# Two-tile feed-forward boundary and transferred head parts in a two-layer fp32 kernel on one core

## The chip, the cores and the metric

The kernel is one program on one core of a Trainium2 chip. Its five instruction streams are TensorE (PE: matmuls, with weight loads shown apart as PEld), VectorE (DVE), ScalarE (ACT), GpSimd (POOL) and SyncE (SP, which here only starts transfers). Each takes its instructions in the order in which they stand in its queue. The metric is the device time of one execution in microseconds, the median of the runs.

## The reference

Two layers over 512 tokens of width 1024, batch 1, in fp32:

```
for layer in 0, 1:
    a = rmsnorm(h, g); mem_n = rmsnorm(mem, g)              # mem: 256 rows
    layer 0: main = gelu(u) * spatial(layernorm(gelu(v)))   # u, v, q_mem = a @ w_in_a; 128-token chunks, 6 groups
    layer 1: k, v, log_f = rmsnorm(h, g) @ w_shared_kv      # 12 heads of 64, causal, blocks of 128 queries
             p = softmax(q k^T / 8 + c_t - c_s), c = cumsum(log_sigmoid(log_f + b)); main = p v
    memory:  4 heads of 64 attend to the 256 rows of mem_n @ w_mem_kv
    h = h + rmsnorm(concat(main, memory) @ w_out, g)
    f = rmsnorm(h, g)
    h = h + rmsnorm((silu(f @ w_gate) * (f @ w_up)) @ w_down, g)   # hidden width 2816 = 22 tiles of 128
```

## The kernel before

Activations lie transposed: `h` is [128, 8, 512], eight tiles of 128 features by 512 tokens. A product in fp32 accuracy is made of three matmuls: each operand is split into a high and a low part (`split`: ScalarE casts the high part, VectorE subtracts it for the low part; with a fourth argument GpSimd subtracts instead), and `mm3` issues high·high, low·high and high·low, which are the profile's lines L174, L175 and L176. Weights come in pieces of 512 KB (`raw`, four buffers, started from SyncE's queue) and are split into `whi` and `wlo` (eight buffers each). PSUM accumulators have three buffers under the tag mm, three under lg, two under tr.

A scheduler orders each engine's queue by the program's text and by when buffers come free. The stages follow each other: layer A's mixing; a boundary; layer A's feed-forward part; a boundary; layer B's projections; its 4 memory heads and 12 forgetting heads (`attend`); a boundary; layer B's feed-forward part; the end.

**A boundary** (`boundary`) ends one residual step and begins the next product. For each half of the tokens (`HALVES`, 256 columns each) it transposes the result `y` (`yt`, L738), adds it to `h` (`residual`), makes the scaled high and low parts of one tile at a time (`normed_parts`: `xshi` on ScalarE, `xslo` by L228 on VectorE), and squares a pair of tiles (`PairNorm.pair`: `sq`, L292, and additions, L294). `Norm.finish` forms the mean square of each token by matmuls of a squared tile with a column `avg` (`st`, L265) and GpSimd raises it to the power -1/2 (`r`, L237). `spread` broadcasts `r` by two matmuls with the identity (`rb`, L233) and copies it to `rbc` (L280). The products of the next step (`group`, accumulators `ps`) run on the unnormalised parts meanwhile; `rbc` scales their results when they are evacuated. In a feed-forward part this is `hidden` for the first two of the 22 hidden tiles: `gr` = gate × `rbc` (L958, VectorE), SiLU (L960, ScalarE), `f` = up × SiLU (L962, VectorE), and the split into `fhi` and `flo`. `close` is spread and evacuation of the second half.

**The feed-forward part** does the other 20 hidden tiles by Strassen's scheme in Winograd's form (`Seven`: seven products of quadrants for eight). `combined` makes the sums of input quadrants that it needs (t3, d2, t4 and d1), after which the first down product `y` (L174 to L176 with a moving width of 512) uses the two plain tiles `fs` with weights from `down_weights`. Before, that part is written in this order:

```
a, close = boundary(phase, G_MIX_POST + layer, G_FFN_PRE + layer, nnorm, rb, first, evac_first)
xs, last = combined(a, G_FFN_PRE + layer, xp)
close()
last()
ys = [[plain("y") for _ in range(2)] for _ in range(TB)]
w = [down_weights(layer, 0, dh) for dh in range(2)]
```

**Layer B's heads.** `Softmax.weigh` takes a block's maximum and exponential with the sum, `norm` scales one block of 128 queries (reciprocal L418, L419: `mp` for memory heads, `p` for the others), `turn` transposes blocks and splits them (`pT`), `join` puts the two heads of a pair into one tile of features (`mixed`, split head by head, L397 and L398). A forgetting head multiplies stacked operands: `qa` and `ka` hold high and low halves above each other, `qc` and `kc` the remaining parts and two rows of the cumulative bias each. `head_parts` makes them for each head from half-height tiles of `q` and `k`, with casts on ScalarE (L1185 and others) and VectorE (`qc`, L1190), subtractions on GpSimd, and two small transfers (L1179, L1180). GpSimd also subtracts for the weights of keys and values in layer B (`prepared(..., G ...)`) and for the heads' values. The keys of the memory reach the other half of the partitions by a transfer of GpSimd's queue (`memk`).

## Time and profile before

| | us |
|---|---|
| median of 3 runs (1162.25 to 1165.3) | 1164.44 |
| profiled execution, its time | 1163.55 |
| its span in the trace | 1161.8 |
| TensorE busy | 1127.2 (97%) |
| VectorE busy | 910.3 (78%) |
| ScalarE busy | 673.4 (58%) |
| GpSimd busy | 89.8 (8%) |

Mean granted clock of TensorE: 0.992 of full speed. The stages by the time from the span's start, with TensorE's and VectorE's busy time in them: layer A's mixing 0 to 165 (156.0 and 124.7 us); boundary 165 to 225 (56.7 and 50.0); feed-forward part 225 to 535 (309.3 and 248.5); boundary 535 to 575 (39.0 and 31.7); projections of layer B 575 to 610 (35.0 and 18.6); heads 610 to 765 (144.9 and 132.3); tail of the mixing 765 to 785 (20.0 and 9.3); boundary 785 to 835 (46.7 and 41.7); feed-forward part 835 to 1140 (304.9 and 240.9); end 1140 to 1162 (14.5 and 12.4).

How the quoted rows read. A group row gives line, engine, operation, output <- inputs, partitions x elements, count (x), then busy us and mean ns of one, then idle time of the engine before it and what ended it. A window row gives start:end, its length, busy us (and count) of PE, PEld, DVE, ACT and POOL, then the granted clock, the share of the DMA engines and GB/s. A timeline row gives start and length in us, then the instructions; the bracket is the wait before them, and its releaser. In a row of transfers the last number is us from issue to landing; where it has three durations they are the issue's minimum, median and maximum in ns.

### The profile page before, as it was taken

The numbers are of one execution on the slowest core, as the hardware profiler recorded it, in microseconds if no ns is written. First come the engines' busy times: TensorE is split into PE (matmuls) and PEld (weight loads), VectorE is DVE, ScalarE is ACT, GpSimd is POOL, SyncE is SP. The second block draws the span as 40 slices with busy tenths as digits, with TensorE's granted clock in tenths as the row PEclk, the third lists the DMA queues.
The fourth block names the chain that finished last, engine by engine and source line by source line (L and its number), as shares of the span: only waits on it lengthen the run. The fifth ranks groups of instructions, "written<-read, shape, count | busy, mean of one in ns | idle before, by whom it ended". The sixth has DMA issues, their size and how long they took to land.

```text
span 1161.8 us, 19755 instructions
## 1 busy us (share of the span) xinstructions
PE 1127.2 (97%) x7485; PEld 1027.0 (88%) x7485; DVE 910.3 (78%) x1783; ACT 673.4 (58%) x1401; POOL 89.8 (8%) x96
## 2 busy tenths in 40 slices
PE   7999999999999999999998999999999999999997
PEld 6898889899899898998987887789799899899996
DVE  7989557898698587897657889857898589678775
ACT  6675466565365263567546788866666256345454
POOL 0000000000000000000024552300000000000000
PEclk9999999999999999999999999999999999999999
DMA  8313221424134223352221111121134233324222
GB/s 290 121 37 109 91 73 37 143 82 157 55 109 146 72 75 109 108 175 84 90 73 56 56 38 58 36 91 37 37 112 148 68 109 110 109 74 145 73 74 73
DMA packets 58183, 108.69 MB, mean 94 GB/s; under 512 B 4013, under 2 KB 38841, under 8 KB 58089
## 3 DMA queue, kind: packets, MB, share of 16 engines
q1 hardware_dynamic: 57624, 106.87, 28.6%
q8 instruction: 59, 0.97, 0.3%
q0 software_dynamic: 320, 0.52, 0.2%
q14 instruction: 36, 0.29, 0.1%
q10 hardware_dynamic: 144, 0.05, 0.0%
HBM read 104.71 MB, written 2.10 MB: 92 GB/s over the span
## 4 chain that ended last, share of the span: by engine, by line
PE 77%; DVE 12%; ACT 7%; issue 2%; DMA 1%; POOL 1%; POOLq 0%; DVEq 0%; ACTq 0%; SPq 0%
PE y L174 8%; PE y L176 8%; PE y L175 8%; PE a L175 4%; PE a L174 4%; PE a L176 4%; PE ps L176 3%; PE ps L175 3%; PE ps L174 3%; PE x L174 3%; PE x L175 3%; PE x L176 3%; PE e L174 3%; PE e L176 3%; PE e L175 3%
## 5 line engine op out<-in xcount | busy, mean ns | idle before, releaser
L222 ACT CAST whi<-raw 128x512 fp32r<-128x512 f32 x460 | 278.6, 620 | 278.8 <-PE y L176 110.9
L223 DVE TENSOR_TENSOR wlo<-raw,whi 128x512 fp32r<-128x512 f32 x442 | 295.3, 686 | 113.1 <-ACT whi L222 108.5
L174 PE MATMUL y<-whi,fhi 128*128 128x512 f32 x352 | 139.3, 399 | 3.8 <-DVE gr L958 2.8
L175 PE MATMUL y<-wlo,fhi 128*128 128x512 f32 x352 | 138.3, 394 | 0.5 <-DVE wlo L223 0.5
L176 PE MATMUL y<-whi,flo 128*128 128x512 f32 x352 | 138.1, 393 | 0.1
L174 PE MATMUL x<-xshi,whi 128*128 128x256 f32 x320 | 90.5, 283 | 0.0
L175 PE MATMUL x<-xslo,whi 128*128 128x256 f32 x320 | 90.5, 283 | 0.0
L175 PE MATMUL a<-xslo,whi 128*128 128x256 f32 x320 | 90.5, 283 | 0.0
L176 PE MATMUL x<-xshi,wlo 128*128 128x256 f32 x320 | 90.5, 283 | 0.0
L174 PE MATMUL a<-xshi,whi 128*128 128x256 f32 x320 | 90.5, 283 | 0.0
L176 PE MATMUL a<-xshi,wlo 128*128 128x256 f32 x320 | 90.4, 283 | 0.0
L174 PEld LDWEIGHTS y<-whi,fhi 128*128 128x128 f32 x352 | 66.8, 190 | 20.7 <-DVE gr L958 3.6
L175 PEld LDWEIGHTS y<-wlo,fhi 128*128 128x128 f32 x352 | 67.0, 190 | 14.8 <-DVE wlo L223 1.6
L176 PEld LDWEIGHTS y<-whi,flo 128*128 128x128 f32 x352 | 66.7, 190 | 15.1 <-DVE flo L223 1.1
L174 PE MATMUL ps<-xshi,whi 128*128 128x256 f32 (+1 forms) x224 | 68.5, 306 | 0.0
L176 PE MATMUL ps<-xshi,wlo 128*128 128x256 f32 (+1 forms) x224 | 67.7, 302 | 0.0
L175 PE MATMUL ps<-xslo,whi 128*128 128x256 f32 (+1 forms) x224 | 67.3, 300 | 0.0
L175 PEld LDWEIGHTS a<-xslo,whi 128*128 128x128 f32 x320 | 61.4, 192 | 0.3
L174 PEld LDWEIGHTS a<-xshi,whi 128*128 128x128 f32 x320 | 61.4, 192 | 0.3
L176 PEld LDWEIGHTS x<-xshi,wlo 128*128 128x128 f32 x320 | 61.3, 192 | 0.0
L176 PEld LDWEIGHTS a<-xshi,wlo 128*128 128x128 f32 x320 | 61.3, 192 | 0.0
L175 PEld LDWEIGHTS x<-xslo,whi 128*128 128x128 f32 x320 | 61.3, 192 | 0.0
(287 smaller groups left out, 3235.4 us busy)
## 6 DMA issues: line engine op xcount, KB each, us to landing
raw<-in_w_gate SPq DMA_DIRECT2D x44, 512.0 KB
raw<-in_w_up SPq DMA_DIRECT2D x44, 512.0 KB
raw<-in_w_down SPq DMA_DIRECT2D x44, 512.0 KB
raw<-in_w_out SPq DMA_DIRECT2D x16, 512.0 KB
raw<-in_w_b_q SPq DMA_DIRECT2D x8, 512.0 KB
raw<-in_w_a_v SPq DMA_DIRECT2D x6, 512.0 KB
raw<-in_w_a_u SPq DMA_DIRECT2D x6, 512.0 KB
raw<-in_w_v SPq DMA_DIRECT2D x6, 512.0 KB
```

Source lines behind the costliest of these rows:

```text
L174: PE.matmul(o, w[0], x[0], start=start, stop=False, skip_group_check=more)
L175: PE.matmul(o, w[0], x[1], start=False, stop=False, skip_group_check=more)
L176: PE.matmul(o, w[1], x[0], start=False, stop=stop, skip_group_check=more)
L222: A.copy(hi, src)
L223: (eng or V).tensor_sub(lo, src, hi)
```

## The change

Seven edits.

1. `PairNorm` adds all four squared pairs into one, so `finish` multiplies two squared tiles for a block of tokens instead of four.
2. The feed-forward boundaries work on two tiles at a time: ScalarE writes the scaled pair in fp32 (`hs`, two activations), then one full-width split makes its parts. Layer B's boundary keeps single tiles. In all boundaries `finish` of the second half moves between the two groups of products.
3. `down_weights` for the first down product and `close` move ahead of `combined`, and `combined` works in place on the scaled pairs, two tiles wide, with its own parts t3, d2 and t4.
4. `join` collects both heads of a pair in one fp32 tile and splits it once, full height.
5. `Softmax.norm` takes two blocks' reciprocals in one instruction and scales both then.
6. The transfer of `memk` reads and writes the same bytes as fp32.
7. In layer B the subtractions of GpSimd (weights, values, queries, keys) go to VectorE; the queries and keys of two heads are split at once (`pair_split`), and six transfers of 64x512 for each head on SyncE's queue stack the parts.

SyncE's queue goes from 234 rows to 294, GpSimd's from 89 to 35, VectorE's from 1729 to 1664, ScalarE's from 1292 to 1242, TensorE's from 7304 to 7286.

TensorE's queue in the first feed-forward boundary, where the products of the second half end (`ps`) and the first down product (`y`) begins, with the broadcast `rb` of the second half. Before:

```order
L174 MATMUL ps_2294<-xshi_1777,whi_2053 128x256
L175 MATMUL ps_2294<-xslo_1778,whi_2053 128x256
L176 MATMUL ps_2294<-xshi_1777,wlo_2054 128x256
L265 MATMUL st_2343<-avg,sq_2108 128x1 x2
L265 MATMUL st_2343<-avg,sq_2121 128x1 x2
L265 MATMUL st_2343<-avg,sq_2108 128x1 x2
L265 MATMUL st_2343<-avg,sq_2121 128x1 x2
L174 MATMUL y_2475<-whi_2457,fhi_1759 128x512
L175 MATMUL y_2475<-wlo_2458,fhi_1759 128x512
L176 MATMUL y_2475<-whi_2457,flo_1760 128x512
L233 MATMUL rb_2419<-ident,r_3_1758 128x128 x2
L174 MATMUL y_2475<-whi_2461,fhi_1761 128x512
```

After:

```order
L174 MATMUL ps_2296<-xshi_2178,whi_2038 128x256
L175 MATMUL ps_2296<-xslo_2179,whi_2038 128x256
L176 MATMUL ps_2296<-xshi_2178,wlo_2039 128x256
L233 MATMUL rb_2365<-ident,r_3_1746 128x128 x2
L174 MATMUL y_2429<-whi_2347,fhi_1747 128x512
L175 MATMUL y_2429<-wlo_2348,fhi_1747 128x512
L176 MATMUL y_2429<-whi_2347,flo_1748 128x512
```

The row sums `st` stand earlier, before the last two groups of products, and the broadcast stands ahead of the first `y` instead of behind three of its matmuls.

ScalarE's queue at the same place, around the load of the SiLU table (`whi` from `raw` are the down weights; `silu` is of the first half). Before:

```order
L292 ACTIVATE sq_2184<-h 128x512
L222 CAST whi_2457<-raw_2455 128x512
L960 ACT_TABLE_LOAD
L960 ACTIVATE silu_2229<-gr_2227 128x256
L222 CAST t_1_2362<-t_2_2364 128x256
L828 ACTIVATE b_2_2373<-h,gains 128x256
L222 CAST fhi_1759<-f_2231 128x256
L960 ACTIVATE silu_2237<-gr_2235 128x256
```

After:

```order
L292 ACTIVATE sq_2182<-h 128x512
L222 CAST xshi_2178<-hs_2175 128x512
L222 CAST whi_2347<-raw_2345 128x512
L222 CAST whi_2351<-raw_2345 128x512
L965 ACT_TABLE_LOAD
L965 ACTIVATE silu_2223<-gr_2221 128x256
L222 CAST whi_2357<-raw_2355 128x512
L222 CAST whi_2361<-raw_2355 128x512
L222 CAST fhi_1747<-f_2225 128x256
```

A second piece of the down weights stands ahead of the table load, two more right behind the first SiLU, and the casts of `combined` are gone from here.

VectorE's queue at the same place, from the copy of the second half's broadcast (`rbc`) on. Before:

```order
L280 COPY rbc<-rb_2419 128x256
L839 SCALAR_TENSOR_TENSOR td_2409<-h,minus_2355,d_2_2390 128x256
L958 TENSOR_TENSOR gr_2423<-ps_2243,rbc 128x256
L839 SCALAR_TENSOR_TENSOR t_8_2410<-h,minus_2355,td_2409 128x256
L223 TENSOR_TENSOR td_lo_2407<-td_2409,td_hi_2406 128x512
L223 TENSOR_TENSOR t_7_2408<-t_8_2410,t_7_2408 128x256
L962 TENSOR_TENSOR f_2427<-ps_2244,silu_2425 128x256
```

After:

```order
L280 COPY rbc<-rb_2365 128x256
L223 TENSOR_TENSOR t_2_2398<-hs_1955,t_1_2397 128x512
L963 TENSOR_TENSOR gr_2369<-ps_2237,rbc 128x256
L223 TENSOR_TENSOR t3lo_2404<-hs_2105,t3hi_2403 128x512
L852 SCALAR_TENSOR_TENSOR hs_1992<-hs_2175,hs_1992 128x512
L967 TENSOR_TENSOR f_2373<-ps_2238,silu_2371 128x256
```

Between `gr` and `f` stand two full-width steps of `combined` instead of one full and two half ones.

SyncE's queue in layer B, between two loads of key weights (`w_k`). Before:

```order
L135 DMA raw_8175<-in_w_k 128x1024
L135 DMA raw_8329<-in_w_k 128x1024
L1179 DMA qc_7123<-cc 2x512
L1180 DMA kc_7125<-cc 2x512
L150 DMA raw_8623<-in_w_out 128x4x256
```

After:

```order
L135 DMA raw_8121<-in_w_k 128x1024
L1194 DMA qc_7071<-whi_7642 64x512
L1194 DMA kc_7073<-wlo_7645 64x512
L1195 DMA qc_7071<-cc 2x512
L1196 DMA kc_7073<-cc 2x512
L1194 DMA qa_7666<-whi_7642 64x512
L1194 DMA qa_7666<-wlo_7643 64x512
L1194 DMA ka_7667<-whi_7644 64x512 x2
L135 DMA raw_8279<-in_w_k 128x1024
```

Each head's two bias transfers are now among eight, and the next load of key weights stands behind them.

The diff, cut to its core:

```diff
-            if j > 1:
-                V.tensor_add(self.sq[j - 2, cols], self.sq[j - 2, cols], self.sq[j, cols])
+            if j:
+                V.tensor_add(self.sq[0, cols], self.sq[0, cols], self.sq[j, cols])
...
-            return [self.sq[j, cols][:, x, c] for j in range(2) for x in range(2)]
+            return [self.sq[0, cols][:, x, c] for x in range(2)]
...
-        own, _ = rows(j)
-        f = temp("f")
+            f = joined[m] = temp("f", tag="acc", bufs=2)
+        else:
+            f = temp("f")
         A.copy(f[:64, :], o[64:, :])
-        V.tensor_add(f[own, :], o[:64, :], f[:64, :])
-        hi, lo = mixed[m]
-        def rest():
-            A.copy(hi[own, :], f[own, :])
-            V.tensor_sub(lo[own, :], f[own, :], hi[own, :])
-        return rest
+        V.tensor_add(joined[m][own, :], o[:64, :], f[:64, :])
+        if j:
+            return lambda: split(joined[m], *mixed[m])
 
...
         def norm(self, tb):
-            c, p = slice(tb, tb + 1), self.p[tb]
-            V.reciprocal(self.sm[:, c], self.sm[:, c])
-            V.tensor_scalar_mul(p, p, self.sm[:, c])
+            if tb % 2:
+                return
+            V.reciprocal(self.sm[:, tb : tb + 2], self.sm[:, tb : tb + 2])
+            for x in (tb + 1, tb):
+                V.tensor_scalar_mul(self.p[x], self.p[x], self.sm[:, x : x + 1])
 
         def turn(self, n, pieces):
...
                 for x in range(2):
-                    k = 2 * j + x
-                    residual(tr[:, 256 * x : 256 * x + 256], k, cols, post)
-                    normed_parts(pre, k, cols, *xs[k])
+                    residual(tr[:, 256 * x : 256 * x + 256], 2 * j + x, cols, post)
+                    if scaled is None:
+                        normed_parts(pre, 2 * j + x, cols, *xs[2 * j + x])
+                if scaled is not None:
+                    scaled[j, half] = plain("hs", (P, 2, 256))
+                    for x in range(2):
+                        A.activation(scaled[j, half][:, x, :], h[:, 2 * j + x, c0:c1], AF.Copy,
+                                     scale=gain(pre, 2 * j + x))
+                    xs[j, half] = pair_parts("xs", scaled[j, half])
                 nnorm.pair(j, cols)
+        def inputs(half):
+            if scaled is not None:
+                return [tuple(t[:, k % 2, :] for t in xs[k // 2, half]) for k in range(KT)]
+            c0, c1 = HALVES[half]
+            return [tuple(t[:, c0:c1] for t in xs[k]) for k in range(KT)]
...
-        outs = group(ws, xs, h0, ["mm", "lg"] * 2, lag=4,
+        outs = group(ws, inputs(0), h0, ["mm", "lg"] * 2, lag=4,
                      after={3: lambda: turn(1, range(2)), 5: lambda: turn(1, range(2, 4))})
         nnorm.finish(h0)
         nnorm.spread(h0, dst)
         evac(outs, h0)
-        outs = group(ws[:2], xs, h1, ["mm", "lg"])
-        outs += group(ws[2:], xs, h1, ["mm", "lg"])
+        outs = group(ws[:2], inputs(1), h0, ["mm", "lg"])
         nnorm.finish(h1)
+        outs += group(ws[2:], inputs(1), h0, ["mm", "lg"])
...
-    def combined(a, pre, xp):
...
-            def from_h(o, x, g, y):
-                V.scalar_tensor_tensor(out=o, in0=x, scalar=g, in1=y, op0=ALU.mult, op1=ALU.subtract)
-            from_h(f[:, 0, :], h[:, n + k, c1], gain(pre, n + k), b12)
-            from_h(d, h[:, k, c0], gain(pre, k), b12)
-            from_h(f[:, 1, :], h[:, n + k, c1], less, d)
-            from_h(f4, h[:, n + k, c0], less, f[:, 1, :])
-            split(f, hi, lo)
...
+    def pair_parts(s, src, room=None):
+        hi, lo = room or [act(f"{s}{n}", shape=(P, 2, 256)) for n in ("hi", "lo")]
+        split(src, hi, lo)
+        return hi, lo
...
+    def combined(xs, scaled, xp):
+        t3, d2, t4 = [], [], []
+        for j in range(2):
+            b11, b12, b21, b22 = (scaled[x] for x in ((j, 0), (j, 1), (j + 2, 0), (j + 2, 1)))
+            V.tensor_sub(b11, b11, b12)
+            V.tensor_sub(b12, b22, b12)
+            t3.append(pair_parts("t3", b12))
+            V.scalar_tensor_tensor(out=b22, in0=b11, scalar=-1.0, in1=b22, op0=ALU.mult, op1=ALU.subtract)
+            d2.append(pair_parts("d2", b22))
+            V.scalar_tensor_tensor(out=b21, in0=b22, scalar=-1.0, in1=b21, op0=ALU.mult, op1=ALU.subtract)
+            t4.append(pair_parts("t4", b21, [xp.tile([P, 2, 256], F32R, tag="t4", name=name("t4")) for _ in range(2)]))
 
         def end():
-            for k, d in enumerate(ones):
-                split(d, *(x[:, c1] for x in a[k]))
-        quadrant = lambda k0, c: [(x[0][:, c], x[1][:, c]) for x in a[k0 : k0 + n]]
-        return (quadrant(0, c0), t3, quadrant(n, c0), d2, t4, quadrant(n, c1), quadrant(0, c1)), end
+            for j in range(2):
+                split(scaled[j, 0], *xs[j, 1])
...
+        halves = lambda pairs: [tuple(t[:, x, :] for t in p) for p in pairs for x in range(2)]
+        quadrant = lambda j, half: halves([xs[j, half], xs[j + 1, half]])
+        return (quadrant(0, 0), halves(t3), quadrant(2, 0), halves(d2), halves(t4), quadrant(2, 1), quadrant(0, 1)), end
...
-        a, close = boundary(phase, G_MIX_POST + layer, G_FFN_PRE + layer, nnorm, rb, first, evac_first)
-        xs, last = combined(a, G_FFN_PRE + layer, xp)
+        scaled = {}
+        a, close = boundary(phase, G_MIX_POST + layer, G_FFN_PRE + layer, nnorm, rb, first, evac_first, scaled)
+        w = [down_weights(layer, 0, dh) for dh in range(2)]
         close()
+        xs, last = combined(a, scaled, xp)
         last()
...
-        w = [down_weights(layer, 0, dh) for dh in range(2)]
...
-                w.extend(prepared(i["w_k"][m], (KT, P), G if m else None))
+                w.extend(prepared(i["w_k"][m], (KT, P)))
...
-                    w.extend(prepared(i["w_v"][j, kh], (4, 256), G if j else None))
+                    w.extend(prepared(i["w_v"][j, kh], (4, 256)))
...
+        def pair_split(pr):
+            pair["q"], pair["k"] = pair_of_parts(), pair_of_parts()
+            split(qs[pr], *pair["q"])
+            split(keys[pr], *pair["k"])
...
             own, other = rows(u.j)
-            q, k = qs[u.pr], keys[u.pr]
...
             u.parts = qa, qc, ka, kc = act("qa"), qc, act("ka"), kc
...
-                A.copy(qa[own, :], q[own, :])
-                G.tensor_sub(qa[other, :], q[own, :], qa[own, :])
...
-                G.tensor_sub(kc[:64, :], k[own, :], ka[own, :])
...
-                V.tensor_copy(qc[:64, :], q[own, :])
...
+            (qh, ql), (kh, kl) = pair["q"], pair["k"]
+            for dst, src in ((qa[own, :], qh), (qa[other, :], ql), (ka[own, :], kh), (ka[other, :], kh),
+                             (qc[:64, :], qh), (kc[:64, :], kl)):
+                nc.sync.dma_start(dst.bitcast(F32), src[own, :].bitcast(F32))
+            nc.sync.dma_start(qc[66:68, :].bitcast(F32), cc[n : n + 33 : 32, :].bitcast(F32))
+            nc.sync.dma_start(kc[64:66, :].bitcast(F32), cc[64 + n : 64 + n + 33 : 32, :].bitcast(F32))
...
-                    split(src.rearrange("p a (b c) -> p a b c", b=2), dst[:, :, :, 0, :], dst[:, :, :, 1, :], G)
...
-            before[len(heads) - 1] = [ready, lambda chunks=chunks: chunks[1](), lambda chunks=chunks: chunks[2]()]
-            if j == 0:
-                before[len(heads) - 1].append(values)
...
+                    split(src.rearrange("p a (b c) -> p a b c", b=2), dst[:, :, :, 0, :], dst[:, :, :, 1, :])
+            make = lambda u=u, n=n: head_parts(u, n)
+            before[len(heads) - 1] = [make] if j else [lambda pr=pr: pair_split(pr), make, values]
```

More of the change, by code (lines that the diff above doesn't have):

```diff
@@ L363, in mem_project @@
                 if layer:
-                    G.dma_start(both[other, :, :], both[own, :, :])
+                    G.dma_start(both[other, :, :].bitcast(F32), both[own, :, :].bitcast(F32))
                 else:
@@ L772, in mix_tail, with boundary @@
         return tail_of([mixed[k] for k in ORDER[4:]], lambda kp, dh, aside: out_weights(layer, 2 + kp, dh, aside), ys)
-    def boundary(phase, post, pre, nnorm, dst, block, evac):
+    def boundary(phase, post, pre, nnorm, dst, block, evac, scaled=None):
         tail, ys = phase
-        xs = parts("xs")
         h0, h1 = HALVES
+        xs = {} if scaled is not None else parts("xs")
         def turn(half, pairs):
@@ L814, in boundary @@
         return xs, close
-    def combined(a, pre, xp):
-        n = KT // 2
-        c0, c1 = (slice(*c) for c in HALVES)
-        minus = xp.tile([P, KT], F32, tag="minus", name=name("minus"), bufs=1)
-        V.tensor_scalar_mul(minus, gains[:, pre * KT : (pre + 1) * KT], -1.0)
-        t3, d2, t4, ones = [], [], [], []
-        for k in range(n):
-            b12 = temp("b12", (P, 256), "sq", 3)
-            A.activation(b12, h[:, k, c1], AF.Copy, scale=gain(pre, k))
-            if k % 2 == 0:
-                d1 = plain("d1", (P, 2, 256))
-            d = d1[:, k % 2, :]
-            ones.append(d)
-            hi, lo = act("td_hi", shape=(P, 2, 256)), act("td_lo", shape=(P, 2, 256))
-            last = xp.tile([P, 2, 256], F32R, tag="t4", name=name("t4"))
-            f, f4 = prob("td", (P, 2, 256)), temp("t4", (P, 256), "sq", 3)
-            less = minus[:, n + k : n + k + 1]
-            def from_h(o, x, g, y):
-                V.scalar_tensor_tensor(out=o, in0=x, scalar=g, in1=y, op0=ALU.mult, op1=ALU.subtract)
-            from_h(f[:, 0, :], h[:, n + k, c1], gain(pre, n + k), b12)
-            from_h(d, h[:, k, c0], gain(pre, k), b12)
-            from_h(f[:, 1, :], h[:, n + k, c1], less, d)
-            from_h(f4, h[:, n + k, c0], less, f[:, 1, :])
-            split(f, hi, lo)
-            split(f4, last[:, 0, :], last[:, 1, :])
-            t3.append((hi[:, 0, :], lo[:, 0, :]))
-            d2.append((hi[:, 1, :], lo[:, 1, :]))
-            t4.append((last[:, 0, :], last[:, 1, :]))
-        def end():
-            for k, d in enumerate(ones):
-                split(d, *(x[:, c1] for x in a[k]))
-        quadrant = lambda k0, c: [(x[0][:, c], x[1][:, c]) for x in a[k0 : k0 + n]]
-        return (quadrant(0, c0), t3, quadrant(n, c0), d2, t4, quadrant(n, c1), quadrant(0, c1)), end
@@ L1197, in layer_b @@
             u = FoxHead(pr, j, split_vals[pr % 2], mixed)
-            chunks = []
-            def ready(u=u, n=n, chunks=chunks):
-                chunks.extend(head_parts(u, n))
-                chunks[0]()
             def values(u=u):
```

11 lines of the change are left out of this document (3 added, 8 removed).

## The prediction

> **What bounds the kernel.** I read the page first, then the span cut into stages, then in the stages that the change touches TensorE's waits and the engines' order of time.
>
> ```profile
> PE 1127.2 (97%) x7485; PEld 1027.0 (88%) x7485; DVE 910.3 (78%) x1783; ACT 673.4 (58%) x1401; POOL 89.8 (8%) x96
> ```
>
> TensorE is busy 97% of the span, so only two things shorten the kernel: less TensorE work, or fewer of its 34.6 us of gaps (span 1161.8 less busy). A stage shows gaps where PE is below the first number of its row; the column after POOL is the granted clock.
>
> ```profile
> 203.00:210.00 7.00, 4.67 (x16) 3.05 (x16) 7.00 (x19) 3.62 (x9) 0.47 (x1) 0.85 0.01 2
> 210.00:225.00 15.00, 15.00 (x90) 13.40 (x90) 11.74 (x23) 9.19 (x18) 0.00 (x0) 0.95 0.49 140
> ...
> 600.00:620.00 20.00, 16.66 (x126) 15.01 (x124) 11.97 (x32) 11.44 (x25) 6.68 (x7) 1.00 0.16 52
> 620.00:640.00 20.00, 19.80 (x107) 17.30 (x108) 15.15 (x39) 13.74 (x35) 7.59 (x7) 0.91 0.18 58
> ...
> 680.00:700.00 20.00, 18.88 (x147) 17.81 (x146) 17.52 (x43) 16.43 (x41) 7.31 (x7) 1.00 0.03 9
> 700.00:720.00 20.00, 17.73 (x100) 14.60 (x100) 18.63 (x44) 16.76 (x40) 7.25 (x6) 1.00 0.24 80
> 720.00:740.00 20.00, 18.49 (x105) 15.20 (x104) 18.68 (x50) 16.36 (x43) 6.77 (x6) 1.00 0.10 28
> ...
> 824.00:835.00 11.00, 8.68 (x30) 6.24 (x30) 11.00 (x25) 4.89 (x12) 0.50 (x1) 0.84 0.25 79
> ```
>
> The gaps sit where the change works: 2.33 us at the end of each feed-forward boundary (203 to 210, 824 to 835), with VectorE busy without a break; 3.34 us where layer B's attention starts (600 to 620); and 4.9 us in the forgetting heads between 680 and 740.
>
> **The boundaries.** The row sums first. `finish` takes four squares a block of tokens now, and two afterwards.
>
> ```profile
> L265 PE MATMUL st<-avg,sq 128*128 128x1 f32 x96 | 11.1, 245 | 0.0
> L294 DVE TENSOR_TENSOR sq<-sq,sq 128x512 f32<-128x512 f32 x12 | 8.2, 686 | 0.0
> L228 DVE SCALAR_TENSOR_TENSOR xslo<-h,gains,xshi 128x256 fp32r<-128x256 f32 x48 | 22.5, 479 | 0.6 <-ACT xshi L227 0.2
> PE rb L233 <- POOL r L237: 2.6, 6, 0.5
> ```
>
> These 96 are the three boundaries' alone; half of them go: **-5.5 us**, all TensorE's own time. The price is a third addition of 686 ns in each of six halves on VectorE, 4.1 us; they lie under the products of the same halves. The rows' scale `r` is then waited for less: TensorE now reaches the broadcast 0.5 us too early six times (one of them in layer A, 2.6 us in all). The order puts 11 instead of 5 products of some 0.12 us between the sums and the broadcast of the first half, and a whole group ahead of that of the second: **-2.0 us**.
>
> Next the stall behind the second half.
>
> ```profile
> 203.53 0.71 PE L233 MATMUL rb<-ident,r 128*128 128x128 f32 x4 [0.40 <-POOL r L237]
> ...
> 206.10 0.50 PE L174 MATMUL y<-whi,fhi 128*128 128x512 f32 x1 [1.40 <-DVE gr L958]
> ...
> 207.82 1.23 PE L174 MATMUL y<-whi,fhi 128*128 128x512 f32 x2 [0.53 <-DVE f L962]
> ...
> 209.28 0.63 PE L176 MATMUL y<-whi,flo 128*128 128x512 f32 x1
> ...
> 205.63 0.41 DVE L958 TENSOR_TENSOR gr<-ps,rbc 128x256 f32<-128x256 f32 x1
> ...
> 206.27 0.41 ACT L960 ACTIVATE silu<-gr 128x256 f32<-128x256 f32 x1
> ```
>
> `gr` and `f` empty the accumulators that the next `y` takes, and they stand in VectorE's queue among the quadrant sums of `combined`; the low parts of the down weights stand behind them. Now the weights are split before the close, so 12 products of 0.23 us (2.7 us) can run on the two free accumulators and six more once `gr` is done, while copy, `gr`, SiLU and `f` (some 0.4 us each) need about 3 us with two full splits of 0.67 us between them, so that `f` is done before those 18 are. The two waits go: 1.93 us twice, **-3.9 us**. The clock goes with them: products at 209 last 0.63 instead of 0.40 us, and the granted clock of 0.85 over 7 us and 0.95 over 15 us is 1.8 us lost, 0.84 over 11 us in the other boundary as much again: **-3.5 us**.
>
> The Trainium skill, "TensorE: Matmul & The Clock Gate", section "Why this matters for your kernels", gives idle gaps of over about 3 us as what costs the clock; these gaps are 1.40 and 0.53 us, and the clock fell, so the trace differs. By that rule the stall would cost its length alone, the clock term would be nothing, and the forecast 3.5 us later.
>
> New waits are my estimate:
>
> ```profile
> 176.32 1.34 ACT L731 ACTIVATE y<-y,r 128x512 f32<-128x512 f32 x2 [0.37 <-POOL r L237]
> 177.09 0.98 PE L738 MATMUL yt<-ident,y 128*128 128x128 f32 x7 [0.46 <-ACT y L731]
> 191.56 0.62 ACT L222 CAST whi<-raw 128x512 fp32r<-128x512 f32 x1 [4.16 <-PE ps L175]
> 192.20 1.28 ACT L960 ACT_TABLE_LOAD   x1
> ```
>
> The transposes of the second half come some 1.2 us earlier in TensorE's order, while ScalarE's scaling of `y` moves forward by perhaps 0.7: +0.5. A second weight split now stands ahead of the SiLU table load. Its slot comes free only when TensorE has ended the first pair of blocks, as the 4.16 us wait shows for the split that stands there today; behind it come 0.62 + 1.28 + two steps of 0.42, against some 2.1 us of work that TensorE has ready: +0.7. The split itself takes two full-width steps (ScalarE 0.5 + 0.5 + 0.62, VectorE 0.69) where one tile had two of 0.49: +0.4 until the first products. So +1.6 in each feed-forward boundary, +0.4 in layer B's: **+3.6 us** (ends 0 and 8).
>
> VectorE's sum for one boundary falls: 16 `xslo` of 479 ns (7.7 us) become 8 subtractions of 686 (5.5), a third addition in each half comes on top (+1.4), and `combined` with its splits takes 16 full-width steps of about 0.7 (11 us) for 24 half-width and 4 full ones (14 us). But the lead that it has when the Strassen products start shrinks:
>
> ```profile
> 217.55 0.69 DVE L881 TENSOR_TENSOR s<-raw,raw 128x512 f32<-128x512 f32 x1 [2.57 <-DMA raw<-in_w_up]
> 230.72 0.69 DVE L881 TENSOR_TENSOR s<-raw,raw 128x512 f32<-128x512 f32 x1 [2.22 <-DMA raw<-in_w_gate]
> 235.00:240.00 5.00, 5.00 (x45) 5.00 (x44) 5.00 (x10) 2.41 (x6) 0.00 (x0) 1.00 0.11 16
> ```
>
> From 231 on VectorE has no gap, so whatever TensorE gains before, VectorE must gain too, or it is given back. It can: it waited 2.57 and 2.22 us for weights whose loads wait for buffers that the late split of the down weights holds, and that split moves forward by some 10 us. I give back **+1.0 us** for both (ends 0 and 7, which is the stall and clock terms whole).
>
> **Layer B.** VectorE takes over GpSimd's subtractions and the heads' splits:
>
> ```profile
> L223 POOL TENSOR_TENSOR wlo<-raw,whi 128x512 fp32r<-128x512 f32 x18 | 23.5, 1320 | 25.2 <-ACT whi L222 19.9 <-PE tr L426 3.0 <-issue 2.2
> L223 DVE TENSOR_TENSOR pT<-tr,pT 128x256 fp32r<-128x256 f32 x12 | 4.9, 412 | 0.0
> L398 DVE TENSOR_TENSOR mixedlo<-f,mixedhi 64x512 fp32r<-64x512 f32 x20 | 16.2, 811 | 4.0 <-ACT mixedhi L397 3.5
> L1190 DVE CAST qc<-q 64x512 fp32r<-64x512 f32 x12 | 9.5, 794 | 0.2
> L1185 ACT CAST ka<-k 64x512 fp32r<-64x512 f32 x12 | 7.4, 616 | 0.0
> 616.23 2.56 DVE L419 TENSOR_SCALAR mp<-mp,sm 128x256 f32<-128x256 f32 x2
> 614.75 5.15 POOL L223 TENSOR_TENSOR wlo<-raw,whi 128x512 fp32r<-128x512 f32 x4 [4.59 <-ACT whi L222]
> 620.20 0.63 PE L426 MATMUL tr<-ident,mp 128*128 128x128 f32 x4 [2.54 <-DVE mp L419]
> 710.24 0.33 PE L473 MATMUL lg<-ka,qa 128*128 128x128 f32 x1 [1.30 <-ACT p L413]
> ```
>
> Added to VectorE: 18 weight subtractions (0.67 us each by their spacing, 12.0), 12 of the values at 0.41 (4.9), 12 of queries and keys (8.0): 24.9 us. Taken off: the twelve `qc` casts (9.5), sixteen half-height `mixedlo` for eight full ones (13.0 to 5.4), 32 of 64 reciprocals at some 0.15 (5.0), and about 2.8 us by which scalings stood still beside GpSimd (two of them took 2.56 us while four GpSimd subtractions ran). That is 24.9 as well: VectorE's load stays, without such standstills. ScalarE loses 36 half-height casts and the half of `mixedhi` and gains 12: about 20 us less.
>
> So at the start of the attention the 2.54 us wait behind `mp` goes, with the slow clock after it (0.91 over 20 us): -2.5 and -1.4, **-3.9 us**. In the heads, 1.30 us at 710 is ScalarE's backlog of such casts and goes; other gaps are the softmax's own latency with VectorE over 90% busy from 700 to 740, and normalising two blocks at once puts one more scaling (0.4 us) ahead of the transposes. Of 4.9 us I take half: **-2.4 us**. The ends: all of it gone (-4.9), or the 8.0 us of new splits wholly on the path (+8.0).
>
> The parts now reach the heads by eight transfers a head on SyncE's queue. The nearest rows:
>
> ```profile
> memk<-memk POOLq DMA_DIRECT2D x4, 128.0 KB, 2.8
> L1179 SPq DMA_DIRECT2D qc<-cc x12: 472/490/579, 612.5 to 737.2; - x12
> ```
>
> Eight issues of 0.49 us and 2.8 us to land are 6.7 us, below the 10 us of a head (twelve heads from 612 to 737), and the splits stand a head and a half ahead in the order: nothing on the path. Layer A's heads get the paired scaling and the joined split too, the memory keys' transfer moves the same bytes, and GpSimd's queue keeps only `r`: nothing each. Weight loads behind the parts in SyncE's queue are asked for early enough (their buffers free a head before use): nothing.
>
> Sum: -5.5 - 2.0 - 3.9 - 3.5 + 3.6 + 1.0 - 3.9 - 2.4 = -16.6. The profiled execution took 1163.55 us (span 1161.8), 0.9 below the median of 1164.44: 1163.55 - 16.6 = 1147; with the median as base 1148. I say **1147**.
>
> **Rivals.** (1) *The boundaries' gain is given back to VectorE.* TensorE reaches the Strassen products earlier, VectorE doesn't, and stalls come at 240 to 255 instead. For it: its unbroken busy time there; against: the 4.8 us of waits on loads that go. Stall and clock terms lost: 1147 + 7 = 1154. (2) *VectorE binds the heads.* Its load is the same on paper, but the new splits fall between softmax steps: +8.0 for -2.4, 1157. (3) *Transfers late: slower than before.* If SyncE, which takes its queue in order, holds a head's parts behind a weight load that waits for a buffer, each of 12 heads waits. It decides from over 10 us between a split and the last landing (I have 6.7 plus what stands ahead); at 2 us beyond, 24 us: 1147 + 2 + 24 = 1173. Against it: splits a head and a half early. (4) *It does nothing in sum*: half the terms hold and the new waits reach their end (8 for 3.6) beside (1): about 1162. (5) *The clock stays low*: other short gaps, as the new waits, hold it down as before, and only idle time returns: 1147 + 3.5 = 1150.5; against it, 0.85 stands only where gaps of over a microsecond are. This is what the rule on the clock gives.
>
> **How the numbers follow.** Forecast 0.54 (own range 1140 to 1151), (1) 0.17, (2) 0.12, (3) 0.06, (4) 0.07, (5) 0.04. The range 1138 to 1158 leaves out (3), (4) and a little of (2) above, some 15 in a hundred, and less than 5 below, where even heads without gaps and no new waits end (1147 - 2.5 - 3.6 - 1 = 1140). 0.3% is about what a measurement of this kernel tells from no change, 3.5 us: faster 0.87, same 0.07, slower 0.06.
>
> **What would show it.** `st` at half its count; no wait for `gr` and `f` at the boundary's end and a clock of 1.00 there; `mp` scalings all near 0.35 us; no gap above 1 us at 600 to 620 but the table load's. Wrong: waits of TensorE for `wlo` or `s` some 30 us behind a boundary, for a transfer at `lg`, or a VectorE without gaps in the heads.

## The result and the profile after

The changed kernel takes 1135.2 us (median of 4 runs, 1134.6 to 1135.97) against 1164.82 for the kernel before: a ratio of 0.975, interval 0.9733 to 0.9767, 29.6 us less. The forecast of 1147 (1138 to 1158) had the direction and little over half the size. The profiled execution took 1135.76 (span 1134.0), 27.8 less than the one before; that is the difference taken apart here.

The page's first line of the changed kernel, its row sums, and its windows where the boundaries of both feed-forward parts end (PE, PEld, DVE, ACT, POOL busy, then the clock):

```profile
PE 1112.0 (98%) x7437; PEld 1018.8 (90%) x7437; DVE 897.7 (79%) x1727; ACT 657.4 (58%) x1367; POOL 24.1 (2%) x42
...
L265 PE MATMUL st<-avg,sq 128*128 128x1 f32 x48 | 5.7, 240 | 0.0
...
188.00:200.00 12.00, 12.00 (x101) 11.80 (x101) 9.94 (x22) 8.66 (x16) 1.69 (x2) 1.00 0.20 53
200.00:213.00 13.00, 13.00 (x68) 11.09 (x67) 12.61 (x25) 8.68 (x19) 0.00 (x0) 1.00 0.34 116
...
785.00:800.00 15.00, 15.00 (x128) 14.80 (x126) 12.94 (x27) 11.02 (x22) 1.72 (x2) 1.00 0.22 71
800.00:811.00 11.00, 11.00 (x51) 9.09 (x50) 10.62 (x22) 6.82 (x14) 0.00 (x0) 1.00 0.00 1
```

TensorE's busy time fell by 15.2 us and its gaps from 34.6 to 22.0. The row sums are at half their count, and TensorE has no gap and full clock through both stretches where it had 2.33 us of gaps each and a clock of 0.85 and 0.84.

To see where the time went, the two traces are laid side by side at the same instructions of TensorE (first `yt` of a boundary, first Strassen product `a`, first product `f` of layer B's projections, first `mlg`, first `lg`):

| stretch | before | after | difference | forecast |
|---|---|---|---|---|
| layer A, to the first `yt` | 164.8 | 165.9 | +1.1 | 0 |
| first feed-forward boundary | 53.7 | 46.9 | -6.8 | |
| boundary to layer B | 59.8 | 57.0 | -2.8 | |
| second feed-forward boundary | 55.3 | 46.9 | -8.4 | |
| three boundaries together | | | -18.0 | -11.3 |
| both Strassen parts | 619.4 | 620.7 | +1.3 | +1.0 |
| memory heads of layer B | 34.8 | 30.6 | -4.2 | -3.9 |
| forgetting heads and mix tail | 138.7 | 130.3 | -8.4 | -2.4 |

With 30.1 against 30.1 us in the two stretches left out, this is 28.2 us to the last matmul. Two rows miss: the boundaries by 6.7 us, the forgetting heads by 6.0. The first row is no effect of the change: over the twenty profiles of this case it runs from 164.3 to 166.0.

### The profile page after: what moved, and what is told of

It reads as the page before. It is cut to its first block, busy times and chain, and to the rows that moved or that the text cites. A ratio compares the mean times of both kernels' runs of the same rounds, so it can differ in the third digit from the quotient of the medians.

```text
span 1134.0 us, 19608 instructions
## 1 busy us (share of the span) xinstructions
PE 1112.0 (98%) x7437; PEld 1018.8 (90%) x7437; DVE 897.7 (79%) x1727; ACT 657.4 (58%) x1367; POOL 24.1 (2%) x42
## 4 chain that ended last, share of the span: by engine, by line
PE 83%; DVE 8%; ACT 4%; DMA 2%; issue 2%; POOL 0%; SPq 0%; POOLq 0%; DVEq 0%; ACTq 0%
PE y L176 8%; PE y L175 8%; PE y L174 8%; PE a L175 5%; PE a L174 5%; PE a L176 5%; PE ps L174 4%; PE ps L175 4%; PE ps L176 4%; PE e L174 3%; PE e L176 3%; PE e L175 3%; PE x L176 3%; PE x L175 3%; PE x L174 3%
## 5 line engine op out<-in xcount | busy, mean ns | idle before, releaser
L223 DVE TENSOR_TENSOR wlo<-raw,whi 128x512 fp32r<-128x512 f32 x460 | 306.4, 686 | 114.6 <-ACT whi L222 110.3
L174 PEld LDWEIGHTS x<-xshi,whi 128*128 128x128 f32 x320 | 61.4, 192 | 0.0
```

What stands on the lines that cost most here:

```text
L174: PE.matmul(o, w[0], x[0], start=start, stop=False, skip_group_check=more)
L223: (eng or V).tensor_sub(lo, src, hi)
```

## What lowers the clock

The trace of the kernel before has four intervals in its body with a granted clock of exactly half, each 3.41 us long. Windows cut at their edges, three of them with the 3.41 us ahead of each:

```profile
204.56:207.97 3.41, 1.48 (x6) 0.82 (x5) 3.41 (x10) 1.81 (x5) 0.00 (x0) 1.00 0.00 0
207.97:211.38 3.41, 3.41 (x8) 2.52 (x9) 3.41 (x9) 1.04 (x3) 0.00 (x0) 0.50 0.22 52
211.38:214.79 3.41, 3.41 (x16) 2.82 (x15) 3.41 (x7) 2.12 (x4) 0.00 (x0) 1.00 0.92 237
617.57:620.98 3.41, 0.87 (x8) 0.81 (x8) 2.45 (x4) 0.85 (x4) 3.41 (x4) 1.00 0.56 161
620.98:624.39 3.41, 3.41 (x12) 2.87 (x11) 2.56 (x6) 1.67 (x5) 0.34 (x1) 0.50 0.40 151
805.31:808.72 3.41, 2.91 (x25) 2.70 (x25) 1.89 (x6) 1.03 (x2) 0.87 (x1) 1.00 0.00 0
808.72:812.13 3.41, 3.41 (x17) 3.41 (x17) 1.73 (x5) 0.00 (x0) 0.00 (x0) 0.50 0.02 5
```

Their starts (207.97, 620.98, 808.72, 829.20) lie 121.0, 55.0 and 6.0 times 3.413 us apart: a fixed grid. An interval at half clock takes 1.7 us of streaming from TensorE, and the four take 6.8; the changed kernel's body has none. The third is the one that the forecast didn't see: TensorE was 85% busy ahead of it, but with 16 `st` matmuls of one column (1.8 us) and a wait for `r` of 0.5. What counts is streamed columns. By the spacing of products (0.120 us for 256 columns, 0.227 for 512) a column takes 0.42 ns. Counted so from every TensorE row of the 20 profiles of this case, all 58 stretches of the grid at full clock that were followed by half clock had TensorE streaming at most 0.38 of the stretch. Of some 6500 that were followed by full clock about ten had 0.36 or less, so the rule has exceptions. At half clock it came back behind stretches of 0.40 and more.

The Trainium skill, "TensorE: Matmul & The Clock Gate", section "What's actually happening", has a window of 4096 cycles, 3413 ns, that runs freely; the distances agree. Its rule in "Why this matters for your kernels", idle gaps of over some 3 us, does not: 1.9 us of waits, or 1.8 us of one-column matmuls and 0.5 of waiting, were enough here.

Where the grid falls is chance, so the number of slow intervals differs from run to run: the 15 runs of the kernel before beside the first experiments have mean clocks of 0.990 to 0.997 and times of 1161.65 to 1168.03. Among them a run that lost 1 us more to the clock (its span times what its clock is short of 1) took some 0.5 us longer, not 1 us; why only half of it shows is open.

## The experiments

Each run has runs of the kernel before on the same chip beside it, whose median lay between 1164.06 and 1166.86. The difference from that is the number to compare with the -29.6 of the full change; stretches are from the profiles.

| run | us | to the kernel before | ratio, interval |
|---|---|---|---|
| row sums alone | 1151.85 | -12.2 | 0.9882 to 0.9913 |
| heads alone | 1155.81 | -8.3 | 0.9913 to 0.9940 |
| boundaries alone | 1154.29 | -9.8 | 0.9908 to 0.9937 |
| order alone | 1160.80 | -3.3 | 0.9951 to 0.9982 |
| old scaling | 1135.78 | -29.8 | 0.9730 to 0.9764 |
| old join | 1140.61 | -25.0 | 0.9774 to 0.9808 |
| GpSimd for weights and values | 1140.37 | -25.2 | 0.9769 to 0.9808 |
| parts head by head | 1143.96 | -21.6 | 0.9801 to 0.9835 |
| the same, moved together | 1145.43 | -20.5 | 0.9813 to 0.9854 |
| old row sums | 1143.88 | -23.0 | 0.9790 to 0.9831 |
| old width | 1135.75 | -29.9 | 0.9733 to 0.9772 |
| one sum more | 1134.03 | -31.6 | 0.9716 to 0.9755 |
| spare casts, ScalarE | 1137.14 | -28.5 | 0.9747 to 0.9784 |
| spare casts, VectorE | 1136.76 | -28.8 | 0.9742 to 0.9782 |
| spare casts, both | 1137.90 | -28.0 | 0.9768 to 0.9789 |

**Row sums alone** (the kernel before with edit 1).

```diff
-            if j > 1:
-                V.tensor_add(self.sq[j - 2, cols], self.sq[j - 2, cols], self.sq[j, cols])
+            if j:
+                V.tensor_add(self.sq[0, cols], self.sq[0, cols], self.sq[j, cols])
...
-            return [self.sq[j, cols][:, x, c] for j in range(2) for x in range(2)]
+            return [self.sq[0, cols][:, x, c] for x in range(2)]
```

> The kernel before with the change of the row sums alone (one sum of four squared pairs, two matmuls a block of tokens). Theory (each part brings what its stage shows): 48 matmuls of 0.112 us go, 5.4 us; the two matmuls' worth of third additions hide. 1164.8 - 5.4 = 1159.4; if the slow clock of 0.86 behind the sums of the second feed-forward boundary goes too, 1157.7. Rival (VectorE takes it back: a third addition of 0.69 us stands ahead of each sum): the waits for the sums or for r grow by as much, 1163 to 1165.

12.2 us, more than either. The boundaries shrink by 3.9, 2.8 and 5.6 us, and the profile has no slow interval in the body, though the standstill of `gr` and `f` is still there:

```profile
198.86:202.27 3.41, 3.07 (x17) 2.07 (x16) 2.31 (x7) 1.71 (x5) 0.87 (x1) 1.00 0.00 0
202.27:205.68 3.41, 1.90 (x7) 1.23 (x7) 3.41 (x10) 2.16 (x6) 0.00 (x0) 1.00 0.00 0
205.68:209.10 3.42, 3.33 (x13) 2.20 (x13) 3.42 (x9) 0.97 (x3) 0.00 (x0) 1.00 0.02 5
```

The edges of the grid cut the same idle time so that TensorE streams for 0.44 of the poorest stretch there, against 0.29 before; in the second feed-forward boundary it is 0.38, at the edge. Part of that is luck of the grid. What isn't is that the sums leave half as much for the waits to add to, and that TensorE's waits for `r` at the boundaries fell too, from 2.3 us to 0.4. So the 12.2 us are not the sums' own time alone: 5.4 are, 1.9 are waits for `r`, and the clock took 3.2 us from these runs in the mean, against 7.4 from those of the kernel before.

**Old row sums** (the changed kernel without edit 1).

> The changed kernel with the old row sums (two sums of squared pairs, four matmuls a block of tokens). Theory W: the 48 matmuls cost their 5.4 us and no more, since with no wait for r beside them 1.8 us of sums leave TensorE streaming for over a third of any stretch of 3.41 us: 1140.6, and no slow stretch at the boundaries. Rival (the sums by themselves bring the slow clock back): one or two slow stretches of 1.7 us at each of three boundaries, 1144 to 1148.

6.6 us above the full change; in its profile the three boundaries are 9.7 longer, 5.4 for the matmuls themselves and two slow intervals. Ahead of both slow intervals TensorE is busy for 90% and more and streams for 0.36 and 0.29 of the stretch:

```profile
186.82:190.23 3.41, 3.30 (x30) 3.09 (x28) 2.25 (x6) 1.60 (x4) 0.99 (x1) 1.00 0.03 5
190.23:193.64 3.41, 3.41 (x16) 3.41 (x17) 1.60 (x3) 0.03 (x1) 0.00 (x0) 0.50 0.00 0
555.46:558.87 3.41, 3.07 (x27) 2.86 (x25) 1.55 (x5) 1.03 (x2) 0.70 (x1) 1.00 0.00 0
558.87:562.28 3.41, 3.25 (x15) 3.25 (x16) 1.99 (x5) 0.52 (x2) 0.11 (x1) 0.50 0.00 0
```

So the sums can bring the slow clock back without any long wait, as the rival has it. But the profiled run is the longest of the four (1145.57 us, mean clock 0.995). The others took 1142.60 to 1144.71 at 0.998, the clock of the full change, so no slow interval fits into their bodies. Measured from the kernel before, theory W stands at -24.2 us and the rival at -20.8 to -16.8. The measured -23.0 is nearer to the theory: in the finished kernel the sums cost little more than their own 5.4 us in most runs.

**Bursts** (behind every pair of Strassen tiles, the output read by nothing).

```diff
+    def short(n):
+        o = ps("tr", (P, 4), s="short")
+        for x in range(n):
+            PE.matmul(o[:, :1], ident, avg, start=x == 0, stop=x == n - 1)
```

> The changed kernel with bursts of one-column matmuls (identity by the column of averages, result read by nothing) behind every pair of Strassen tiles: ten bursts of 28 in the first feed-forward part (3.1 us each), ten of 16 in the second (1.8 us each), 49 us of their own time at 0.112 each. Theory W (the granted clock is halved for 3.41 us after a stretch of a fixed grid of 3.41 us in which TensorE streams columns for less than about a third, and one-column matmuls stream next to nothing): bursts of 16 leave at least 0.47 of any stretch, so no slow clock behind them; bursts of 28 leave under a third in about six cases of ten: some six slow stretches in the first part, 1.7 us each. Time 1135 + 49 + 10 = 1194. Rival (a matmul counts as work whatever its width; only standstill lowers the clock): no slow stretch, 1184.

1302.5 us in one run. Each call shows as two rows (880 for 440 calls), so the bursts were twice as long as planned, 4.2 us for the shorter ones, and the numbers expected don't hold; the question is answered all the same. All 20 bursts are followed by half clock, though TensorE never stands still in them:

```profile
938.50:941.95 3.45, 3.45 (x34) 3.45 (x32) 3.45 (x8) 2.15 (x4) 0.00 (x0) 1.00 0.00 0
941.95:948.78 6.83, 6.83 (x33) 6.83 (x34) 3.32 (x6) 1.71 (x4) 0.00 (x0) 0.50 0.22 79
```

So the rival, that any matmul counts as work, falls.

**Boundaries alone** (edits 2 and 3 on the kernel before, with the old sums).

> The kernel before with the changes of the boundaries alone (two tiles at a time, the second half's sums between the groups, down weights and close ahead of combined, combined in place), with the old row sums. Theory: 2 x 4.9 us of standstill and slow clock at 200 to 215 and 824 to 835 go, the waits for r shrink (some 1.5), the slow clock at 808 to 812 may go (1.7): 1164.8 - 9.8 - 1.5 = 1153.5 (1151.8 with the clock). Rival (the parts need each other: four squares a block delay the sums' end so that r is late again): 1157 to 1159.

Near the theory: the feed-forward boundaries lose 4.9 and 6.4 us, and the one to layer B has a slow interval at 558.5.

**Order alone.**

```diff
+        w = [down_weights(layer, 0, dh) for dh in range(2)]
+        close()
         xs, last = combined(a, G_FFN_PRE + layer, xp)
-        close()
         last()
         ys = [[plain("y") for _ in range(2)] for _ in range(TB)]
-        w = [down_weights(layer, 0, dh) for dh in range(2)]
```

> The kernel before with one edit: the down weights and close stand ahead of combined, which is otherwise the old one, half-width and from h. Theory (the order of the text is what removes the standstill of gr and f): the 2 x 4.8 us at the end of both feed-forward boundaries go, 1155; the later Strassen sums may give 1 to 2 of it back. Rival (the width is what matters: VectorE has 4 us more to do per boundary with the old combined, and it is without a gap from 203 on): the wait moves to the first Strassen products, which wait for t3 and d2: 1160 to 1164.

The time is in the rival's range: the boundaries lose 2.8 and 4.4 us, and the first Strassen part takes 5.1 back, with a slow interval at 281.4. The chain is not the rival's, though; TensorE doesn't wait for t3 or d2. The timeline at the first long down products shows weights that land late, their splits, the sum `s` (L920) behind those in VectorE's queue, then TensorE.

```profile
275.14 1.14 ACT L222 CAST whi<-raw 128x512 fp32r<-128x512 f32 x2 [2.87 <-DMA raw<-in_w_down]
275.80 1.29 DVE L223 TENSOR_TENSOR wlo<-raw,whi 128x512 fp32r<-128x512 f32 x2 [1.92 <-ACT whi L222]
...
280.55 0.50 PE L174 MATMUL y<-whi,fhi 128*128 128x512 f32 x1 [2.33 <-DVE s L920]
```

**Old width** (the changed kernel with single tiles and the old `combined`, but with edit 1 and the new order).

> The changed kernel with the boundaries of the kernel before, one tile at a time, and the old half-width combined, but with the new row sums, the second half's sums between the groups, and down weights and close ahead of combined: what is left out is the width alone. Theory (the order takes the standstill away, the width keeps VectorE from giving it back): as in the run with the order alone, the first long down products wait for weights whose buffers VectorE frees late (there 5.2 us in the first Strassen part): 1140 to 1143. Rival (the width does nothing here, since the row sums' change took the slow stretches): 1135 to 1137.

The rival holds: 29.9 us, the whole gain, with feed-forward boundaries of 46.3 us each against 46.9. Two tiles at a time and the sums in place bring nothing that can be measured once the row sums and the order are changed. What the order alone gave back doesn't recur here either (the first Strassen part takes 320.8 us, there 323.8); why it doesn't wasn't tried by itself.

**Heads alone** (edits 4 to 7 on the kernel before).

> The kernel before with the changes of the heads alone: paired scaling, joined split, no GpSimd subtractions in layer B, queries and keys split by pairs and stacked by transfers. Theory (the parts add): the stages 575 to 785 give what they gave in the full change, 12.6 us: 1152.2. Rival (the heads gain only because the boundaries let them start with loads further ahead): about half, the 6.3 us of the prediction: 1158.5.

8.3 us, between the two: in its profile the memory and forgetting heads lose 4.1 and 7.2, nearly what the full change shows, but five slow intervals stand in its boundaries.

**Old scaling, old join, GpSimd back, head by head** (the changed kernel with one of the heads' edits undone; in the last, `qa`, `kc` and `qc` are made as before, with VectorE in GpSimd's place).

```diff
-                G.tensor_sub(qa[other, :], q[own, :], qa[own, :])
+                V.tensor_sub(qa[other, :], q[own, :], qa[own, :])
...
-                G.tensor_sub(kc[:64, :], k[own, :], ka[own, :])
+                V.tensor_sub(kc[:64, :], k[own, :], ka[own, :])
```

> The changed kernel with the old scaling of one block at a time (a reciprocal for each of 64 blocks). The stretch from the first memory-head product of layer B to the next boundary takes 160.9 us in the changed kernel and 173.4 in the one before; which edit brought the 12.5? Theory G (GpSimd's subtractions were the brake, by their own 1.3 us and by holding VectorE): this edit is worth 0 to 0.5 us: 1135.5. Rival S (the number of small steps on VectorE and ScalarE between the softmax steps was the brake): 32 more reciprocals of some 0.15 us lie on the chain of each head, some 2 us: 1137.

> The changed kernel with the old join (each head's half split by itself). Theory G: 0 to 0.5 us, 1135.5. Rival S: VectorE has eight steps of 0.8 us more for one of 0.69 less a pair (some 7 us in all) and ScalarE as much, a third of it on the path: 1137.5.

> The changed kernel with GpSimd's subtractions put back for layer B's key and value weights and for the heads' values; queries and keys stay split by pairs and stacked by transfers. Theory G: the wait behind the scaling of the memory heads comes back (2.5 us, and 1.7 of slow clock where TensorE streams too little for one 3.41 us stretch), and a part of the heads' waits: 4 to 7 us, 1139 to 1142. Rival S: VectorE has 17 us less to do, so nothing or a gain: 1133 to 1135.

> The changed kernel with the head parts made head by head as before, with casts on ScalarE and VectorE and half-height subtractions, but the subtractions on VectorE, so without GpSimd and without the stacking transfers. Theory G: GpSimd is gone all the same, 0 to 1 us: 1135.5. Rival S: some 22 us of ScalarE's and 15 of VectorE's half-height steps are back in a stretch in which both are over 80% busy: 4 to 6 us, 1140.

The scaling is worth nothing, as theory G said. The other edits divide by place. GpSimd costs 2.8 us at the memory heads (33.4 against 30.6) and 1.2 in the forgetting heads. The mean `mp` scaling is 449 ns before, 349 after and 427 with GpSimd back, and TensorE's wait for it is back:

```profile
L419 DVE TENSOR_SCALAR mp<-mp,sm 128x256 f32<-128x256 f32 x32 | 14.0, 449 | 0.6
...
L422 DVE TENSOR_SCALAR mp<-mp,sm 128x256 f32<-128x256 f32 x32 | 9.8, 349 | 0.3
```

```profile
L422 DVE TENSOR_SCALAR mp<-mp,sm 128x256 f32<-128x256 f32 x32 | 12.3, 427 | 0.5
...
PE tr L429 <- DVE mp L422: 2.7, 1, 2.7
```

In the forgetting heads theory G falls: the old join alone makes them 4.6 us longer and the parts head by head 7.6, without any GpSimd. TensorE's waits there, first with the old join, then head by head:

```profile
PE o L497 <- DVE pT L223: 1.9, 6, 0.5
PE lg L476 <- ACT f L392: 1.2, 1, 1.2
...
PE lg L476 <- ACT p L413: 0.8, 2, 0.4
```

```profile
PE tr L429 <- DVE p L422: 4.5, 6, 1.4
PE tr L429 <- DVE mp L422: 0.7, 1, 0.7
PE o L497 <- DVE pT L223: 0.6, 2, 0.3
```

Together with GpSimd's 1.2 this is more than the 8.4 of the whole, so the kernel before was waiting for several things at once.

**Load or place?** Spare casts load one engine in the heads without being waited for.

```diff
+            before[len(heads) - 1] += [lambda u=heads[-1]: [A.copy(spare, u.parts[0][:64, 256 * x : 256 * x + 256]) for x in range(2)]] * 2 if n else []
```

Their first form read `q`, which is ready long before; all 48 casts ended ahead of the forgetting heads, and those runs (1137.27 and 1137.1, 29.6 and 29.8 under the kernel before) tell nothing:

> The changed kernel with four more casts of 64x256 on ScalarE for each forgetting head, written to a spare tile that nothing reads. Some 0.4 us each, 19 us in all, about what ScalarE lost in the heads by the change. Theory A (ScalarE's queue was what the heads' chain waited for): a good part comes back, 3 to 6 us, 1139 to 1141. Rival V (VectorE's queue was): 0 to 1 us, 1135 to 1136.

> The changed kernel with the same four spare casts of 64x256 for each forgetting head on VectorE instead: 0.4 to 0.5 us each, some 20 us. Theory V: VectorE goes from 88% busy in the heads to nearly 100%, and 5 to 12 us come back: 1140 to 1147. Theory A: 0 to 2 us, 1135 to 1137.

The second form ran inside the heads:

> The changed kernel with four casts of 64x256 on ScalarE for each forgetting head but the first, that read the stacked queries of the head before (so they can't run ahead of the heads, as the spare casts of the last pair did, which ended before 604 us) and write a tile that nothing reads: 44 times 0.4 us, 18 us. Theory A (the heads gained because ScalarE lost 20 us there): 1135.2 + 3 to 6 = 1138 to 1141. Rival V (because VectorE lost 7): 0 to 1 us, 1135 to 1136.

> The changed kernel with the same 44 casts on VectorE: at the 0.29 us that such casts took in the last run, 13 us, twice what VectorE lost in the heads by the change (131.3 to 124.1 us). Theory V: VectorE is at 97% of the heads' 141 us then, 4 to 8 us, 1139 to 1143. Rival A: 0 to 1 us, 1135 to 1136.

> The changed kernel with spare casts on both engines at once in the heads: 44 of 64x256 on ScalarE (17.8 us, which alone cost 1.9) and 66 of 64x128 on VectorE (some 13 us, as much as the 44 of 64x256 that alone cost 1.6). Theory L (the load of both engines together is what the head-by-head parts cost): well over the sum of the two, 5 to 8 us, 1140 to 1143. Rival P (the place of the steps and their length between the softmax steps is): the sum, 3.5 us, 1138.7.

> The kernel with head parts made head by head on ScalarE and VectorE (1143.96), with the same instructions moved: each head's three pieces in one place, and those of a pair's second head right behind the first's, where the changed kernel splits the pair. Theory L: the same load, the same time, 1143 to 1145. Rival P: a good part of the 8.8 us goes, 1138 to 1141.

ScalarE's 17.8 us make the forgetting heads 2.1 us longer, VectorE's 12.2 make them 1.3 longer, both together 2.8 (there VectorE's casts are 66 short ones, 14.1 us). With both, the engines are as busy from 610 to 745 as with the parts made head by head (the first row; DVE and ACT are the third and fourth number behind the length):

```profile
610.00:745.00 135.00, 128.55 (x808) 113.06 (x807) 127.51 (x296) 105.91 (x257) 0.00 (x0) 1.00 0.17 55
```

```profile
610.00:745.00 135.00, 132.49 (x833) 117.07 (x832) 127.64 (x348) 108.14 (x283) 0.00 (x0) 1.00 0.50 126
```

So load explains 2.8 of the 7.6, and theory L falls. Moving the parts together doesn't help either (139.5 us of heads against 137.8), so the rival falls in the form tried. What remains is how the parts themselves tie the engines: casts of 0.62 us and subtractions of 0.69 where the spare casts took 0.2 to 0.4, subtractions that wait for ScalarE's cast, and buffers of `qc` and `kc` that TensorE must have left, all in the queue that the softmax steps use. Which of these it is stays open.

**One sum more** (the changed kernel; the two halves of the sum of squares are added too, and one matmul call a block is left).

> The changed kernel with one step further: the two halves of the sum of squares are added as well (128x256, 0.41 us on VectorE, six times), so that one matmul call a block of tokens is left of two. Theory: 24 of the 48 remaining matmuls of 0.112 us go, 2.7 us, if r isn't late by the added 0.41: 1132.5. Rival (the addition stands in the chain that r waits for): TensorE meets r at the broadcast, 1135 to 1136.

31.6 us under the kernel before. Its profile shows the boundaries at 46.0, 56.5 and 46.0 us, 2.2 less than the full change, near the 2.7 expected. The intervals of the two ratios overlap, so the times alone don't show that it is faster.

## Why the prediction was wrong

The two traces differ by 28.2 us where the forecast had 16.6. Three steps hold 11.1 of the 11.6 us between. The largest is the term of the forgetting heads, forecast at -2.4 and measured at -8.4. The new waits of the boundaries were forecast at +3.6 and measured at +0.2. And a third slow interval of 1.7 us at the boundaries was not read. Term by term:

- *Row sums, -5.5.* 96 rows became 48, as said, and taking the edit out of the full change loses 6.6, near the price. The 12.2 that it brings alone holds waits for `r` and slow intervals too, which the forecast had as terms of their own and which the other edits also remove. What the term left out is that TensorE streams next to nothing under the sums, so that they help to bring the clock down.
- *Waits for `r`, -2.0.* Right: 2.3 us of them are gone, and none is left at the boundaries.
- *Stall on `gr` and `f`, -3.9, and the clock, -3.5.* Both went. The clock term read only the windows behind the stalls; this one, at 803 to 815 in the kernel before, was not read, and holds 1.7 us more:

```profile
803.00:815.00 12.00, 11.50 (x85) 11.29 (x84) 6.64 (x17) 5.12 (x10) 0.87 (x1) 0.86 0.00 1
```

- The forecast was right that the clock falls behind gaps as short as 1.40 and 0.53 us, and its rival (5) fails. Why it falls was not seen: the gaps add up within one stretch of the grid, with the row sums.
- *New waits, +3.6.* Wrong by 3.4 us. Two splits do stand ahead of the table load, but TensorE has no wait from 195 to 206. Only the wait for `yt` grew, by 0.4 us in both feed-forward boundaries together (the row of waits below is of the second, which had 0.4 before), and it fell by 0.2 in layer B's:

```profile
191.62 1.14 ACT L222 CAST whi<-raw 128x512 fp32r<-128x512 f32 x2 [1.89 <-PE ps L175]
192.78 1.28 ACT L965 ACT_TABLE_LOAD   x1
194.08 0.42 ACT L965 ACTIVATE silu<-gr 128x256 f32<-128x256 f32 x1
```

```profile
PE yt L741 <- ACT y L734: 0.7, 1, 0.7
```

- *VectorE's lead, +1.0.* The Strassen parts took 1.3 more. Rival (1) was not what happened here; it is what the order alone did.
- *Memory heads, -3.9.* Measured -4.2, by the mechanism named, as the run with GpSimd put back shows. (A clock of 0.91 over 20 us is 1.8 us, not the 1.4 of the term.)
- *Forgetting heads, -2.4.* The step that failed most: 6.0 us. The term took three windows (680 to 740) with 4.9 us of gaps and halved them. The stage is more than twice as long, and TensorE's waits in it were spread; its waits from 625 to 765 before, and from 612 to 746 after:

```profile
PE lg L473 <- ACT p L413: 2.3, 3, 1.3
PE tr L426 <- DVE p L419: 2.3, 4, 1.1
PE o L494 <- DVE pT L223: 1.7, 4, 0.6
```

```profile
PE tr L429 <- DVE p L422: 0.6, 1, 0.6
PE lg L476 <- ACT p L413: 0.4, 1, 0.4
PE o L497 <- DVE pT L223: 0.2, 1, 0.2
```

  That is 6.3 us against 1.2. The rest is lost between matmuls without a wait that the profile names: counted by the spacing of TensorE's starts over the usual one for each width, the stage lost 9.5 us before and 1.0 after. The forecast called VectorE's load unchanged and gave ScalarE's 20 us no price beyond one wait of 1.30 us. In the whole of the heads both loads fell, as these windows show (before, then after):

```profile
610.90:764.30 153.40, 143.30 (x880) 124.44 (x879) 131.27 (x307) 121.56 (x288) 60.07 (x50) 0.99 0.16 50
```

```profile
603.20:744.10 140.90, 138.67 (x883) 124.03 (x882) 124.08 (x293) 100.83 (x254) 0.00 (x0) 1.00 0.48 121
```

  VectorE lost 7.2 and ScalarE 20.7. But spare casts of about this size (17.8 us on ScalarE, 14.1 on VectorE) cost 2.8 us. So the load that the term weighed is the smaller part. Undone one by one, the joined split is worth 4.6 us here, the parts by pairs 7.6 and GpSimd's subtractions 1.2; the term gave the first two no price of their own. How the parts do it stays open.
- *Transfers, nothing.* Right so far as the trace shows: no product waits for one. Twice as many transfers were not tried.

## What to carry to other kernels

Ask of a TensorE instruction that streams few columns what it does to the clock too: add it to the waits near it, and look at the granted clock window by window through a whole stage, not only behind the largest wait. Where a stage has many short waits, sum them over the stage before taking a share of them, and undo each part in the finished kernel: two parts (the scaling by two, the double width) brought nothing, and one was worth 12.2 us alone but 6.6 in the finished kernel.

## What the hardware showed that was not expected

The clock falls to half in whole stretches of a fixed 3.413 us grid, behind one in which TensorE streamed at most 0.38 of the time (58 of 58 in these traces, though about ten stretches of 0.36 or less were followed by full clock), and it falls while TensorE issues matmuls without a break if they have one column (20 of 20 bursts). One such stretch takes 1.7 us of streaming. How the grid happens to cut the waits differs from run to run: the mean clocks of one program's runs went from 0.990 to 0.997, and their times by 6.4 us.
